# Weights and state-space parameters handed over in the layout in which the kernel loads them

## The chip, the core and the metric

The kernel runs on one core of one Trainium2 chip. The core has a matrix engine (TensorE, PE in the profile, with PEld for its weight loads), a vector engine (VectorE, DVE), a scalar engine (ScalarE, ACT), a general engine (GpSimd, POOL) and a queue engine (SyncE, SP). Sixteen DMA engines move data between HBM and the on-chip memory for the queues that SP, ACT and POOL fill. The metric is the device time of one execution in microseconds (us), the median over the runs.

## The reference, cut to what matters

One layer of a hybrid encoder over 16 meta tokens and 1024 tokens of width 1024, all in float32.

```
xn    = rmsnorm(h)                      # h = [meta; x], 1040 x 1024
proj  = xn @ w_in                       # 1024 x 4104: q 512, k 512, v 512, f 8, u 512, gates 2048
y_a   = forgetting_attention(q, k, v, f + b_forget) @ w_attn_out
z     = gelu(s5(u, lambda, b, c, d, log_dt))   # 32 groups, 64 complex states, 16 channels each
zg    = z @ w_glu ;  y_s = zg[:, :1024] * sigmoid(zg[:, 1024:])
h     = h + (sigmoid(gates_a) * y_a + sigmoid(gates_s) * y_s) @ w_o
hid   = rmsnorm(h) @ w_ffn_up           # 1024 x 5632
conv  = ffn_conv_b + causal depthwise conv of width 3 over hid
h     = h + (silu(conv_gate) * conv_val) @ w_ffn_down
out   = rmsnorm(h)[16:]
```

In the state-space part (S5) `lambda`, `b` and `c` are complex and come as real and imaginary arrays.

## The kernel before, in words

Every float32 product is computed as three products of a reduced-precision pair: an operand is split into `hi` (a cast) and `lo` (the rest, by `split_lo`, L128), and `dense_steps` (L142 to L146) issues hi\*hi, hi\*lo and lo\*hi. A weight chunk of 128 columns is loaded by `wchunk` (L130): one DMA of 512 KB into a tile `[128, 8, 128]`, whose DRAM side is a slice of the weight as the caller gave it, so 1024 pieces of 512 bytes. From `w_in` these pieces lie one row of 4104 floats, 16,416 bytes, apart.

The stages in order, and what of them matters here:

1. **Start (L255 to L302).** SP issues `x` (eight tiles of 512 KB, 4 KB per row), and after the second of them the four loads `uraw` (L288), 512 KB each, which bring the u columns of `w_in` in pieces of 2 KB. POOL loads lambda (`lraw`, four small DMAs, L1251) and `log_dt`. TensorE turns lambda to states-on-partitions (L1258), VectorE copies it out (L1259). ScalarE squares each token tile for its norm, VectorE scales it (L163), TensorE transposes it (L172), ScalarE and VectorE write `xhi` and `xlo` (L174, L128). `u_weights` (L269) splits the u weights on ScalarE and POOL.
2. **State-space stage (L304 to L342, function `ssm`).** A long chain of VectorE instructions builds tables from lambda, b and c; c is loaded in 256-byte pieces (L1267), transposed by eight TensorE instructions (L1452) and copied out by eight VectorE ones (L1455, L1457); b is loaded in 64-byte pieces (L1270, L1271). TensorE works on `u_proj` and on gate chunks (L372) meanwhile.
3. **z, q, k and the forget gate (L376 to L540).** The result of the state-space part goes to DRAM (`y_d`) and comes back (`zt`, L463). The 8 forget columns of `w_in` come as `fraw` (L383), 1024 pieces of 32 bytes, POOL splits them into `wf` (L386), and TensorE uses them at L438.
4. **Attention (L604 to L789).** Per pair of heads; between its products TensorE runs the next pair's q and k projection and gate chunks, whose weights come by `wchunk`. The attention output tile `ob` has one buffer; it is written by VectorE (L703) and stored by SP (L769).
5. Merge, output projection, feed-forward (L796 to L1221). `up_raw` (L926) loads 512 KB chunks of `w_ffn_up`. The convolution's parameters come in three loads, two TensorE transposes and a copy (L900 to L909).

A planner orders the instructions of each engine (`schedule_with_timeline_sim=True` in L1612) by planned times; engines then run their own lists in order, and so do the DMA queues. So a change of loads can also change the order.

Of the kernel before, what the change touches and what calls it, by code (L numbers as in the profile page):

```python
# [9 lines left out]
F = mybir.dt.float32  # L10
# [37 lines left out]
def block_kernel(ctx, tc, x, meta, g1, w_in, b_f, w_ao, l_re, l_im, b_re, b_im, c_re, c_im,  # L48
                 d_sk, l_dt, w_glu, w_o, g2, w_up, cw, cb, w_dn, gf, out, dbg=None, upto=99):
    nc = tc.nc  # L50
    dbg = dbg or {}
    x, g1, w_in, b_f, w_ao = x[0], g1[0], w_in[0], b_f[0], w_ao[0]
    l_re, l_im, b_re, b_im, c_re, c_im = l_re[0], l_im[0], b_re[0], b_im[0], c_re[0], c_im[0]
    d_sk, l_dt, w_glu, w_o, g2 = d_sk[0], l_dt[0], w_glu[0], w_o[0], g2[0]
    w_up, cw, cb, w_dn, out = w_up[0], cw[0], cb[0], w_dn[0], out[0]
# [225 lines left out]
    ssm_log, ssm_loads, ssm_steps = ssm(tc, after, sp, st_ps, ident, u_d, y_d, l_re, l_im, b_re, b_im, c_re, c_im, d_sk, l_dt)  # L281
# [207 lines left out]
    def glu(i):  # L489
# [64 lines left out]
    def value_weights(q):  # L554
# [6 lines left out]
        SY.dma_start(raw, w_in[2 * P * q:2 * P * q + 2 * P, 2 * AW:3 * AW].rearrange("(k p) m -> p k m", p=P))  # L561
# [338 lines left out]
    cwr = fc.tile([P, 2, P], F, name="cwr")  # L900
    cw2 = cw.rearrange("j (m p) -> (j m) p", p=P)
    SY.dma_start(cwr[:, 0], cw2[:P])
    SY.dma_start(cwr[:4, 1], cw2[P:])
    SY.dma_start(cwr[4:48, 1], cb.rearrange("(m p) -> m p", p=P))
    cwt = fc.tile([P, 176], F, name="cwt")
# [318 lines left out]
def ssm(tc, after, sp, s_ps, ident, u_d, y_d, l_re, l_im, b_re, b_im, c_re, c_im, d_sk, l_dt):  # L1224
# [6 lines left out]
    def TS(*a):  # L1231
        log.append(V.tensor_scalar(*a))
# [31 lines left out]
    def loads():  # L1264
        for w, (p0, p1) in enumerate(((c_re, c_im), (c_im, c_re))):
            for i, src in enumerate((p0, p1)):
                SY.dma_start(craw[:, :, w, i, :],  # L1267
                             src.rearrange("g c s -> (g c) s").rearrange("(m p) s -> p m s", p=P))
        for k_, (p0, p1) in enumerate(((b_re, b_im), (b_im, b_re))):
            SY.dma_start(bw[:64, k_], p0.rearrange("g s c -> s g c"))  # L1270
            SY.dma_start(bw[64:, k_], p1.rearrange("g s c -> s g c"))  # L1271
        SY.dma_start(dT, d_sk.rearrange("(g c) -> c g", c=GC))

    def rest():
# [173 lines left out]
        cA, cB = sm([P, G, GC]), sm([P, G, GC])  # L1448
        for mch in range(4):
            for w, dst in enumerate((cA, cB)):  # L1450
                tp = s_ps()
                PE.transpose(tp[:, :P], craw[:, mch, w].rearrange("p i s -> p (i s)"), ident)  # L1452
                dv = dst[:, 8 * mch:8 * mch + 8].rearrange("p g c -> p (g c)")
                if w == 0:
                    TS(dv, tp[:, :P], sg, None, ALU.mult)  # L1455
                else:
                    TS(dv, tp[:, :P], -1.0, None, ALU.mult)  # L1457
# [22 lines left out]
        def tables(qt):  # L1480
# [12 lines left out]
            TT(Gm, Gm, tm, ALU.add)  # L1493
# [122 lines left out]
```

## Time and profile before

| what | us |
|---|---|
| median of 3 runs | 1540.2 (1536.94 to 1541.24) |
| profiled execution, its own time | 1544.01 |
| its span from first to last instruction | 1542.1 |
| TensorE busy in the span | 1464.8 (95%) |
| mean granted TensorE clock | 0.984 of full speed |

The profile is of one execution, 3.8 us above the median of the timed runs. Busy times are read against the span; sums of changes are made against the execution's own time.

### The profile page before, as it was taken

To read this page: it belongs to the slowest core of one execution; us is meant where nothing else is said; L and a number is where in the kernel's file an instruction comes from. 1 tells how busy PE (TensorE), PEld (TensorE's weight loads), DVE (VectorE), ACT (ScalarE), POOL (GpSimd) and SP (SyncE) were. 2 spreads that over 40 slices of the span, in tenths; PEclk is the share of its full clock that TensorE was granted. 3 is DMA by queue.
4 is the path that set the end of the run, shared out by engine and by line. 5 is a ranking of instruction groups with operands and counts; after the bars stand their busy time and mean duration, and the time that the engine had idled before them with its cause. 6 is when DMAs were issued, how large, how long until landed. Compare 5 with 4: busy or idle time off the path is not lost.

```text
span 1542.1 us, 26276 instructions
## 1 busy us (share of the span) xinstructions
PE 1464.8 (95%) x9649; PEld 1373.3 (89%) x9649; DVE 1087.7 (71%) x2226; ACT 666.8 (43%) x1295; POOL 752.2 (49%) x810
## 2 busy tenths in 40 slices
PE   5998998999999989999999989999999999989997
PEld 4998897998899979999778989999999999878886
DVE  5999747882466656656425798888887774788695
ACT  5143456541455646542213444344444443454343
POOL 5332234853445445635201564555544336599766
PEclk9999998999999989999999999999999999999998
DMA  8466472553232233127542045667743224774412
GB/s 208 84 91 102 96 123 48 166 165 68 46 61 53 61 38 74 53 95 245 203 113 92 28 119 150 158 178 181 174 130 103 83 70 164 264 234 140 141 48 109
DMA packets 164450, 183.53 MB, mean 119 GB/s; under 512 B 25257, under 2 KB 120233, under 8 KB 163971
## 3 DMA queue, kind: packets, MB, share of 16 engines
q1 hardware_dynamic: 150883, 155.49, 35.4%
q0 software_dynamic: 7648, 15.78, 7.2%
q10 hardware_dynamic: 5792, 10.60, 1.9%
q8 instruction: 76, 1.25, 0.3%
q14 instruction: 51, 0.42, 0.1%
HBM read 142.76 MB, written 60.96 MB: 132 GB/s over the span
## 4 chain that ended last, share of the span: by engine, by line
PE 61%; DVE 19%; DMA 7%; issue 4%; POOL 4%; ACT 3%; SPq 1%; POOLq 0%; ACTq 0%; DVEq 0%
PE mm L146 4%; PE mm L144 4%; PE mm L145 4%; PE sp L200 3%; PE sp L201 3%; PE sp L202 3%; DVE sw L128 3%; PE tp L677 2%; PE tp L200 2%; PE tp L201 2%; PE tp L202 2%; DVE ov L1028 2%; PE mm L202 2%; PE mm L201 2%; PE mm L200 2%
## 5 line engine op out<-in xcount | busy, mean ns | idle before, releaser
L144 PE MATMUL mm<-xhi,whi 128*128 128x342 f32 (+2 forms) x584 | 192.6, 330 | 1.7 <-DVE q L128 1.0
L146 PE MATMUL mm<-xhi,wlo 128*128 128x342 f32 (+2 forms) x584 | 190.7, 327 | 0.0
L145 PE MATMUL mm<-xlo,whi 128*128 128x342 f32 (+2 forms) x584 | 190.3, 326 | 0.0
L144 PEld LDWEIGHTS mm<-xhi,whi 128*128 128x128 f32 x584 | 111.5, 191 | 3.5 <-ACT xhi L174 1.1
L128 DVE TENSOR_TENSOR sw<-sf,sw 128x512 fp32r<-128x512 f32 x76 | 75.1, 988 | 55.9 <-ACT sw L937 55.9
L968 POOL TENSOR_TENSOR ov<-ov,og 128x1024 f32<-128x1024 f32 x21 | 51.2, 2439 | 124.7 <-ACT og L967 121.9
L145 PEld LDWEIGHTS mm<-xlo,whi 128*128 128x128 f32 x584 | 111.4, 191 | 0.6 <-DVE xlo L128 0.2
L146 PEld LDWEIGHTS mm<-xhi,wlo 128*128 128x128 f32 x584 | 111.2, 191 | 0.6 <-issue 0.2
L128 POOL TENSOR_TENSOR wlo<-raw,whi 128x1024 fp32r<-128x1024 f32 x24 | 62.7, 2615 | 78.5 <-ACT whi L136 78.2
L937 ACT CAST sw<-sf 128x512 fp32r<-128x512 f32 x76 | 47.4, 624 | 117.7 <-POOL sf L945 92.2
L684 ACT CAST th<-tp 128x256 fp32r<-128x256 f32 (+3 forms) x120 | 56.1, 472 | 72.6 <-PE tp L677 29.5
L200 PE MATMUL mm<-xhi,sw 128*128 128x256 f32 (+1 forms) x304 | 85.5, 281 | 0.5 <-DVE ov L992 0.5
L202 PE MATMUL mm<-xhi,sw 128*128 128x256 f32 (+1 forms) x304 | 85.5, 281 | 0.0
L201 PE MATMUL mm<-xlo,sw 128*128 128x256 f32 (+1 forms) x304 | 85.2, 280 | 0.0
L128 DVE TENSOR_TENSOR tl<-tp,th 128x256 fp32r<-128x256 f32 (+3 forms) x120 | 65.2, 547 | 25.5 <-ACT th L684 23.7
L1028 DVE SCALAR_TENSOR_TENSOR ov<-hv,cwt,ov 128x1024 f32<-128x1024 f32 x38 | 77.7, 2043 | 1.9 <-ACT ov L1026 1.8
L945 POOL TENSOR_TENSOR sf<-raw 128x512 f32<-128x512 f32 x38 | 51.2, 1348 | 54.0 <-DVE hv L206 19.5
L945 POOL TENSOR_TENSOR sf<-raw,sf 128x512 f32<-128x512 f32 x38 | 67.1, 1766 | 21.3 <-DVE sw L128 21.3
L937 ACT CAST sw<-raw 128x512 fp32r<-128x512 f32 x69 | 42.4, 619 | 74.4 <-DMA raw<-in_w_ffn_up_dram 35.9
L649 POOL TENSOR_SCALAR pt<-pt,nm 128x144 f32<-128x144 f32 (+4 forms) x72 | 50.9, 709 | 43.6 <-DVE nm L648 42.4
L698 PE MATMUL po<-th,vt 128*128 128x256 f32 (+1 forms) x200 | 57.5, 302 | 7.9 <-DVE nm L645 7.8
L647 ACT ACTIVATE pt<-pt,nm 128x144 f32<-128x144 f32 (+4 forms) x72 | 52.9, 735 | 27.9 <-DVE nm L646 27.3
(603 smaller groups left out, 5467.8 us busy)
## 6 DMA issues: line engine op xcount, KB each, us to landing
raw<-in_w_ffn_up_dram SPq DMA_DIRECT2D x44, 512.0 KB, 4.0
t_d<-in_w_ffn_down_dram POOLq DMA_DIRECT2D x44, 256.0 KB, 6.9
ar<-a_d SPq DMA_DIRECT2D x44, 256.0 KB, 4.6
wr<-t_d SPq DMA_DIRECT2D x44, 256.0 KB, 2.9
a_d<-ov SPq DMA_DIRECT2D x21, 512.0 KB, 2.6
raw<-in_w_in_dram SPq DMA_DIRECT2D x20, 512.0 KB, 7.6
wr<-in_w_ffn_down_dram SPq DMA_DIRECT2D x33, 256.0 KB, 2.9
t_d<-in_w_ffn_down_dram SPq DMA_DIRECT2D x22, 256.0 KB, 4.7
```

What stands on the lines that cost most here:

```text
L128: return eng.tensor_tensor(out_, src, hi.bitcast(F), ALU.subtract)
L144: yield PE.matmul(ps, whi[:, i, :], ahi[:, i], start=(i == 0), stop=False)
L145: yield PE.matmul(ps, whi[:, i, :], alo[:, i], start=False, stop=False)
L146: yield PE.matmul(ps, wlo[:, i, :], ahi[:, i], start=False, stop=(i == k - 1))
L200: PE.matmul(ps, a[0][:, i], bh, start=(i == 0 and not joins), stop=False, skip_group_check=True)
L201: PE.matmul(ps, a[0][:, i], bl, start=False, stop=False, skip_group_check=True)
L202: PE.matmul(ps, a[1][:, i], bh, start=False, stop=(i == kh - 1), skip_group_check=True)
L684: S.copy(th[:kn, z:tw], tp[:kn, z:tw])
L698: PE.matmul(po[:, :w], vt[:kn, kk, h, :], th[:kn, gi * w:gi * w + w], start=(kk == 0), stop=False)
L937: S.copy(hi, src)
L945: sums.append(GP.tensor_tensor(f_, a, b, op))
L1028: V.scalar_tensor_tensor(out=o, in0=h_[:, j:SEQ + j], scalar=cwc(j, m), in1=o, op0=ALU.mult, op1=ALU.add)
```

## The change

The host now lays the inputs out before the kernel's DRAM tensors are made (`_laid_out`). The 128-column weights become blocks `[chunk, 128 partitions, k, 128]`, so a chunk is one run of 4 KB per partition (2 KB for `w_attn_out` and the halves of `w_glu`), 512 KB without gaps. The u and v columns become `[128, 8, 512]`, 16 KB per partition, of which each load takes 4 KB; the forget columns `[128, 8, 8]`. Lambda, b and c come with the states doubled over the 128 partitions, so that they are loaded as they are used, and the transposes of lambda, c and the convolution's parameters go. The sign of the second c array moves into `tables` (ADD becomes SUBTRACT). The lower half of the first u chunk's split moves from POOL to VectorE.

```diff
 def wchunk(src, k, eng=None, act=False):
-        (GP if act else SY).dma_start(raw, src.rearrange("(k p) m -> p k m", p=P))
+        (GP if act else SY).dma_start(raw, src)
...
-            split_lo(GP, lo[:, sl], src, hi[:, sl])
+            split_lo(V if m == 0 else GP, lo[:, sl], src, hi[:, sl])
...
-                SY.dma_start(raw, w_in[2 * P * j:2 * P * j + 2 * P, 3 * AW + H:3 * AW + H + SW]
-                             .rearrange("(k p) m -> p k m", p=P))
+                SY.dma_start(raw, w_u[:, 2 * j:2 * j + 2])
...
-        c0 = 3 * AW + H + SW + P * i
-        whi, wlo = wchunk(w_in[:, c0:c0 + P], KD, GP, act=not tanh)
+        whi, wlo = wchunk(w_g[i], KD, GP, act=not tanh)
...
-        SY.dma_start(fraw, w_in[:, 3 * AW:3 * AW + H].rearrange("(k p) m -> p k m", p=P))
+        SY.dma_start(fraw, w_f)
...
-            whi, wlo = wchunk(w_in[:, w * AW + P * pr:w * AW + P * pr + P], KD, GP)
+            whi, wlo = wchunk((w_q, w_k)[w][pr], KD, GP)
...
-            SY.dma_start(raw[:, 4 * q:4 * q + 4],
-                         w_glu[:, D * q + P * i:D * q + P * i + P].rearrange("(k p) m -> p k m", p=P))
+            SY.dma_start(raw[:, 4 * q:4 * q + 4], w_glu[KD * q + i])
...
-        SY.dma_start(raw, w_in[2 * P * q:2 * P * q + 2 * P, 2 * AW:3 * AW].rearrange("(k p) m -> p k m", p=P))
+        SY.dma_start(raw, w_v[:, 2 * q:2 * q + 2])
...
+            SY.dma_start(raw, w_o[4 * hf + m])
...
+        whi, wlo = wchunk(w_ao[i], 4)
...
-    tp = t_ps()
-    PE.transpose(tp[:, :P], cwr[:, 0], ident)
-    PE.transpose(tp[:, P:P + 48], cwr[:48, 1], ident[:48, :48])
-    V.tensor_copy(cwt, tp[:, :176])
+    cwt = fc.tile([P, 4, 2 * NFF], F, name="cwt")
+    SY.dma_start(cwt, cwt_d)
...
+        SY.dma_start(raw, w_up[m])
...
 def ssm(...):
-    lraw = big("dt8", [P, 2, 2, NS], "lraw")[:G]
-    for i, src in enumerate((l_re, l_im)):
-        for j in range(2):
-            GP.dma_start(lraw[:, i, j, :], src)
...
-    for i in range(2):
-        tp = s_ps()
-        PE.transpose(tp[:, :G], lraw[:, i].rearrange("g a s -> g (a s)"), ident[:G, :G])
-        V.tensor_copy(lam[:, i], tp[:, :G])
-    craw = big("tq", [P, 4, 2, 2, NS], "craw")
+    GP.dma_start(lam, lam_d)
+    cAB = sm([P, 2, G, GC])
...
+        SY.dma_start(cAB, cw_d)
+        SY.dma_start(bw, bw_d)
+        SY.dma_start(dT, d_sk)
...
-        for mch in range(4):
-            for w, dst in enumerate((cA, cB)):
-                tp = s_ps()
-                PE.transpose(tp[:, :P], craw[:, mch, w].rearrange("p i s -> p (i s)"), ident)
...
+        cA, cB = cAB[:, 0], cAB[:, 1]
+        TS(cA, cA, sg, None, ALU.mult)
...
-            TT(Gm, Gm, tm, ALU.add)
+            TT(Gm, Gm, tm, ALU.subtract)
...
+    def by_rows(w):
+        return w.reshape(-1, P, w.shape[1]).transpose(1, 0, 2)
+    def blocks(w):
+        return w.reshape(w.shape[0] // P, P, -1, P).transpose(2, 1, 0, 3)
+    def twice(re, im):
+        return _np.stack([_np.concatenate([re, im]), _np.concatenate([im, re])], axis=1)
```

## Rows read from the trace of the kernel before

**Rows 1.** The page's engines: busy us, share of the span, instructions.

```profile
PE 1464.8 (95%) x9649; PEld 1373.3 (89%) x9649; DVE 1087.7 (71%) x2226; ACT 666.8 (43%) x1295; POOL 752.2 (49%) x810
```

**Rows 2.** Waits of TensorE: for whom, us in total, times, longest us.

```profile
PE sp L1258 <- DMA lraw<-in_ssm_lambda_re_dram: 8.5, 1, 8.5
PE po L698 <- DVE nm L645: 7.8, 2, 6.9
...
PE tp L172 <- DVE sm L1259: 5.6, 1, 5.6
...
PE mm L438 <- DVE q L128: 4.4, 1, 4.4
```

**Rows 3.** Stretches of the start: busy us, instructions, clock, DMA share, GB/s.

```profile
8.00:17.00 9.00, 4.35 (x22) 3.70 (x22) 4.79 (x9) 4.47 (x11) 7.42 (x7) 1.00 0.96 185
17.00:27.00 10.00, 5.04 (x20) 4.42 (x21) 5.12 (x20) 5.78 (x12) 2.78 (x5) 1.00 1.05 367
```

**Rows 4.** The chain that ended last, its first long piece: start, us, what.

```profile
3.76 15.43 DMA uraw<-in_w_in_dram
```

**Rows 5.** Timeline of the start: start us, us, engine, line, what, idle before.

```profile
19.21 0.71 ACT L274 CAST whi<-uraw 128x256 fp32r<-128x256 f32 x2 [2.37 <-DMA uraw<-in_w_in_dram]
...
21.05 0.18 DVE L1259 COPY sm<-tp 128x32 f32<-128x32 f32 x1
...
21.28 1.12 PE L172 MATMUL tp<-ident,xt 128*128 128x128 f32 x4 [5.59 <-DVE sm L1259]
...
23.07 0.82 PE L144 MATMUL mm<-xhi,whi 128*128 128x272 f32 x2 [0.68 <-ACT xhi L174]
```

**Rows 6.** DMA issues from 543 to 558 us: KB each, us to landing.

```profile
raw<-in_w_in_dram SPq DMA_DIRECT2D x1, 512.0 KB, 13.0
o_d<-ob SPq DMA_DIRECT2D x1, 128.0 KB, 10.7
```

**Rows 7.** Timeline of the same stretch: SP's store, VectorE, TensorE.

```profile
547.09 12.99 SPq L769 DMA_DIRECT2D o_d<-ob  x2
...
557.84 0.17 DVE L703 TENSOR_TENSOR ob<-po,ot 64x16 f32<-64x16 f32 x1 [7.20 <-DMA o_d<-ob]
...
558.06 0.38 PE L698 MATMUL po<-th,vt 16*128 16x16 f32 x1 [6.86 <-DVE nm L645]
```

**Rows 8.** Stretches right after two stalls, columns as in rows 3.

```profile
558.00:564.00 6.00, 5.94 (x23) 5.92 (x24) 3.29 (x21) 2.63 (x8) 2.24 (x7) 0.52 0.02 3
...
248.40:256.60 8.20, 7.49 (x28) 6.08 (x29) 7.28 (x13) 7.71 (x19) 4.03 (x5) 0.50 0.07 20
```

**Rows 9.** Timeline around the forget gate: POOL, ACT, PE.

```profile
239.28 4.20 POOL L386 TENSOR_SCALAR wf<-fraw 128x64 fp32r<-128x64 f32 x1 [7.61 <-DMA fraw<-in_w_in_dram]
...
244.78 0.62 ACT L485 CAST z3h<-zf 128x520 fp32r<-128x520 f32 x1 [6.02 <-POOL zf L479]
...
248.41 0.46 PE L438 MATMUL mm<-xhi,wf 128*64 128x272 f32 x1 [4.44 <-DVE q L128]
```

**Rows 10.** The page's DMA issues: count, KB each, median us to landing.

```profile
raw<-in_w_ffn_up_dram SPq DMA_DIRECT2D x44, 512.0 KB, 4.0
...
raw<-in_w_in_dram SPq DMA_DIRECT2D x20, 512.0 KB, 7.6
```

**Rows 11.** Groups of instructions from 40 to 53 us: count, busy us, mean ns, idle.

```profile
L1232 DVE TENSOR_SCALAR sm<-sp,sm 128x128 f32<-128x128 f32 x4 | 1.4, 347 | 0.2 <-PE sp L1452 0.2
...
L1232 DVE TENSOR_SCALAR sm<-tp 128x128 f32<-128x128 f32 x4 | 1.1, 287 | 0.1
...
L1452 PE MATMUL tp<-ident,craw 128*128 128x128 f32 x4 | 1.1, 272 | 0.0
```

**Rows 12.** Single tiles, bw and raw: ns min/median/max, first and last start.

```profile
L1235 DVE TENSOR_TENSOR sm<-bw,sm x2: 678/678/679, 71.5 to 72.2; 128x512 f32<-128x512 f32 x2
...
L128 DVE TENSOR_TENSOR ops<-raw,ops x16: 388/668/941, 246.2 to 328.6; 128x256 fp32r<-128x256 f32 x16
```

**Rows 13.** A stretch of the state-space stage, columns as in rows 3.

```profile
120.00:140.00 20.00, 16.80 (x109) 16.22 (x109) 19.62 (x43) 6.93 (x10) 2.99 (x4) 0.91 0.62 125
```

More of the change, by code (lines that the diff above doesn't have):

```diff
@@ L47, in block_kernel @@
 @with_exitstack
-def block_kernel(ctx, tc, x, meta, g1, w_in, b_f, w_ao, l_re, l_im, b_re, b_im, c_re, c_im,
-                 d_sk, l_dt, w_glu, w_o, g2, w_up, cw, cb, w_dn, gf, out, dbg=None, upto=99):
+def block_kernel(ctx, tc, x, meta, g1, w_q, w_k, w_v, w_f, w_u, w_g, b_f, w_ao, lam_d, bw_d, cw_d,
+                 d_sk, l_dt, w_glu, w_o, g2, w_up, cwt_d, w_dn, gf, out, dbg=None, upto=99):
     nc = tc.nc
     dbg = dbg or {}
[L52 to L55, printed above, removed]
+    out = out[0]
     V, S, GP, PE, SY = nc.vector, nc.scalar, nc.gpsimd, nc.tensor, nc.sync
@@ L280, in block_kernel @@
     S.dma_start(g1B, g1.partition_broadcast(P))
-    ssm_log, ssm_loads, ssm_steps = ssm(tc, after, sp, st_ps, ident, u_d, y_d, l_re, l_im, b_re, b_im, c_re, c_im, d_sk, l_dt)
+    ssm_log, ssm_loads, ssm_steps = ssm(tc, after, sp, st_ps, ident, u_d, y_d, lam_d, bw_d, cw_d, d_sk, l_dt)
     xts = [sp.tile([P, D], F, tag=tag, name="xt", bufs=n) for tag, n in (("sy", 3), ("Gm", 2), ("Wi", 2), ("U", 2))
@@ L804, in wo_half @@
             raw = rp.tile([P, KD, P], F, tag=rtag, name="raw", bufs=1 if rtag == "wraw" else 2)
-            c0 = 512 * hf + P * m
-            SY.dma_start(raw, w_o[:, c0:c0 + P].rearrange("(k p) m -> p k m", p=P))
+            SY.dma_start(raw, w_o[4 * hf + m])
             sl = slice(P * m, P * m + P)
@@ L836, in block_kernel @@
         ga = ga if i < KD - 1 else okeep["g"]
-        whi, wlo = wchunk(w_ao[:, P * i:P * i + P], 4)
+        whi, wlo = wchunk(w_ao[i], 4)
         for t, n in QBLK:
@@ L899, in block_kernel @@
     fc = pool(st_r, "ffnc", side="right")
[L900 to L905, printed above, removed]
-    tp = t_ps()
-    PE.transpose(tp[:, :P], cwr[:, 0], ident)
-    PE.transpose(tp[:, P:P + 48], cwr[:48, 1], ident[:48, :48])
-    V.tensor_copy(cwt, tp[:, :176])
+    cwt = fc.tile([P, 4, 2 * NFF], F, name="cwt")
+    SY.dma_start(cwt, cwt_d)
     def cwc(j, m):
-        return cwt[:, 44 * j + m:44 * j + m + 1]
+        return cwt[:, j, m:m + 1]
     NH = LQ // 2 + 1
@@ L927, in up_raw @@
         raw = rp.tile([P, KD, P], F, tag="raw", name="raw", bufs=3)
-        SY.dma_start(raw, w_up[:, P * m:P * m + P].rearrange("(k p) m -> p k m", p=P))
+        SY.dma_start(raw, w_up[m])
         return raw
@@ L1221, in block_kernel, with ssm @@
         room[0] += len(groups[g])
-def ssm(tc, after, sp, s_ps, ident, u_d, y_d, l_re, l_im, b_re, b_im, c_re, c_im, d_sk, l_dt):
+def ssm(tc, after, sp, s_ps, ident, u_d, y_d, lam_d, bw_d, cw_d, d_sk, l_dt):
     nc = tc.nc
@@ L1264, in loads @@
     def loads():
[L1265 to L1272, printed above, removed]
+        SY.dma_start(cAB, cw_d)
+        SY.dma_start(bw, bw_d)
+        SY.dma_start(dT, d_sk)
     def rest():
@@ L1445, in rest @@
         yield
-        cA, cB = sm([P, G, GC]), sm([P, G, GC])
-        for mch in range(4):
-            for w, dst in enumerate((cA, cB)):
-                tp = s_ps()
-                PE.transpose(tp[:, :P], craw[:, mch, w].rearrange("p i s -> p (i s)"), ident)
[L1453 to L1457, printed above, removed]
+        cA, cB = cAB[:, 0], cAB[:, 1]
+        TS(cA, cA, sg, None, ALU.mult)
         b1, b2 = bw[:, 0], bw[:, 1]
@@ L1587, in ssm, with _laid_out @@
     return log, loads, rest()
-_INS = ["x", "meta_tokens", "norm_mix_g", "w_in", "b_forget", "w_attn_out", "ssm_lambda_re", "ssm_lambda_im",
-        "ssm_b_re", "ssm_b_im", "ssm_c_re", "ssm_c_im", "ssm_d", "ssm_log_dt", "w_glu", "w_o", "norm_ffn_g",
-        "w_ffn_up", "ffn_conv_w", "ffn_conv_b", "w_ffn_down", "norm_final_g"]
 _OUTS = [((1, SEQ, D), "float32")]
+def _laid_out(x, meta_tokens, norm_mix_g, w_in, b_forget, w_attn_out, ssm_lambda_re, ssm_lambda_im, ssm_b_re, ssm_b_im,
+              ssm_c_re, ssm_c_im, ssm_d, ssm_log_dt, w_glu, w_o, norm_ffn_g, w_ffn_up, ffn_conv_w, ffn_conv_b,
+              w_ffn_down, norm_final_g):
+    import numpy as _np
+    def by_rows(w):
[4 more added lines that the diff above has]
+        return _np.stack([_np.concatenate([re, im]), _np.concatenate([im, re])], axis=1)
+    w = w_in[0]
+    q, k, v, f, u, g = _np.split(w, [AW, 2 * AW, 3 * AW, 3 * AW + H, 3 * AW + H + SW], axis=1)
+    lam = _np.stack([ssm_lambda_re[0].T, ssm_lambda_im[0].T], axis=1)
+    conv = _np.concatenate([ffn_conv_w[0], ffn_conv_b], axis=0)
+    return dict(x=x[0], meta=meta_tokens, g1=norm_mix_g[0], w_q=blocks(q), w_k=blocks(k), w_v=by_rows(v),
+                w_f=by_rows(f), w_u=by_rows(u), w_g=blocks(g), b_f=b_forget[0], w_ao=blocks(w_attn_out[0]),
+                lam=_np.concatenate([lam, lam]),
+                bw=twice(ssm_b_re[0].transpose(1, 0, 2), ssm_b_im[0].transpose(1, 0, 2)),
+                cw=twice(ssm_c_re[0].transpose(2, 0, 1), ssm_c_im[0].transpose(2, 0, 1)),
+                d_sk=ssm_d[0].reshape(G, GC).T, l_dt=ssm_log_dt[0], w_glu=blocks(w_glu[0]), w_o=blocks(w_o[0]),
+                g2=norm_ffn_g[0], w_up=blocks(w_ffn_up[0]), cwt=conv.reshape(4, -1, P).transpose(2, 0, 1),
+                w_dn=w_ffn_down[0], gf=norm_final_g)
 def kernel(**inputs):
@@ L1604 @@
     arrays, args = {}, []
-    for name in _INS:
-        a = _np.ascontiguousarray(inputs[name])
+    for name, a in _laid_out(**inputs).items():
+        a = _np.ascontiguousarray(a)
         arrays[f"in_{name}_dram"] = a
```

## The prediction, made before the changed kernel ran

> **What bounds the kernel now.** I read the page's engines first [rows 1]: TensorE is busy 1464.8 of 1542.1 us, so all its idle time is 77 us, and no change of loads can win more than that, plus what the clock loses. So the question is not how many bytes or packets are saved but which of TensorE's pauses end with a load. The list of its waits [rows 2] names only four of 4 us or more that I can tie to this diff: 8.5 us for lambda and 5.6 us for the copy L1259, both at the start, 6.9 us at L698 in attention (the longest of two waits there), 4.4 us at L438. The list says which engine released TensorE, not what that engine had waited for; for that I went to the timeline around each, and to the chain that ended last for the start.
>
> At the start the chain holds one long piece, 15.43 us until the last `uraw` load lands at 19.2 us [rows 4]. The DMA engines are full all the while, but from 8 to 17 us, when u comes, they move 185 GB/s, and from 17 to 27 us, when mostly x follows, 367 [rows 3]. Bytes per time differ by two at the same busy share: it is how the u columns are read that is slow. ScalarE sits until that landing at 19.21 us and VectorE behind it, so the lambda copy runs only at 21.05 us and releases TensorE's transposes at 21.28; the first u product starts at 23.07 us [rows 5].
>
> In attention VectorE waits 7.20 us at L703 for the store of `ob`, which has one buffer, and TensorE 6.86 us behind it [rows 7]. That store, 128 KB, takes 10.7 us to land, and the load from `w_in` that was issued before it on SP takes 13.0 us for 512 KB [rows 6]. The store stands behind a slow load.
>
> At the forget gate POOL waits 7.61 us for `fraw`, spends 4.20 us on L386, and only then forms the sum for which ScalarE has waited 6.02 us; ScalarE's copies of q and VectorE's follow it, and TensorE stands 4.44 us at L438 [rows 9]. After either pause the granted clock is half for a while: 0.52 over 6 us and 0.50 over 8.2 us [rows 8].
>
> Loads from `w_in` are the slow ones: 7.6 us to land for 512 KB in 512-byte pieces, against 4.0 for `w_ffn_up` with the same pieces [rows 10].
>
> **The change part by part.**
>
> *Start.* Four u loads are 2.10 MB. At 185 GB/s that is 11.3 us, at the rate that x gets, 367 GB/s, 5.7 us: 5.6 us less. What is late next is the chain of norm and transposes of the second x tile; with lambda's transposes gone from TensorE and its two copies from VectorE nothing of [rows 5] but ScalarE's casts and `xlo` stands between that landing and the first product, so I let it move by the whole 5.6. The bound below is nothing: u is not contiguous after the change, its 4 KB pieces lie 16 KB apart. The 8.5 us of lambda [rows 2] I count at nothing more: it overlaps the wait for x and the u weights. The DMAs of b and c fall from eight to two and nothing in the list waits for them: zero.
>
> The split of the lower half of the first u chunk on VectorE is four instructions of 128x256. Such cost 0.39 to 0.67 us [rows 12], 1.6 to 2.7 us in all. VectorE is busy 4.79 of 9 us there [rows 3], so I take zero; if u lands in half the time and the cover is gone, 2.7 us at most.
>
> *Transposes.* Eight transposes of c at 0.272 us are at most 2.2 us of TensorE; eight copies on VectorE are 4 x 0.347 + 4 x 0.287 = 2.5 us [rows 11]. One multiply of 128x512 comes in. The trace has none from on-chip memory; bounds are 0.287 (the copy of 128 columns) and 0.678 (a two-operand instruction of that size [rows 12]); I take 0.5. VectorE is full in the stage that follows, 19.62 of 20 us while TensorE has 3.2 us idle [rows 13], so its time there is time of the end: 2.5 - 0.5 = 2.0 us; bounds 0 and 2.5. ADD against SUBTRACT, and the convolution's two transposes and copy far from any wait, are nothing.
>
> *Attention.* The chunk of q, k or gate weights becomes 512 KB without gaps. Even with the 4.0 us of `w_ffn_up`, still in 512-byte pieces in this trace [rows 10], the load issued at 543.5 us is done by 547.5, just after the store was issued at 547.09 us [rows 7], and the store no longer queues behind it. Won: 6.86 us, and of the six us at 0.52 of the clock 6 x 0.48 = 2.9 us [rows 8]; 9.7 together. I take 9.5; bound below 0, if another transfer stands there.
>
> *Forget gate.* `fraw` becomes 128 pieces of 256 bytes. It took 7.4 us from its issue to POOL's start. With 4 us [rows 10] POOL is 3.4 us earlier, and ScalarE and VectorE behind it. That leaves 1 us of the 4.44, and VectorE has work of its own in between. The clock's loss is 8.2 x 0.50 = 4.1 us [rows 8]. Bounds 0 and 8.5; I take 6, most of both.
>
> *Moved or shortened at no price.* The gate chunks' loads on POOL, the halves of `w_glu`, `w_o`, `w_attn_out` and `w_ffn_up` end earlier, but TensorE waits for none of them [rows 2]: zero, and no cover is needed as nothing is added to a queue. No instruction gains a wait that it did not have: each new DMA writes the tile that the old ones wrote.
>
> **Sum.** 5.6 + 2.0 + 9.5 + 6 = 23.1 us from 1544.01 us, the profiled execution's own time: 1520.9. That execution is 3.8 us above the median of 1540.2, inside what pauses of this kind can vary; I give **1520 us**, 1.3% less.
>
> **A rule that speaks against it.** The trace has 512-byte pieces at two speeds, 4.0 and 7.6 us for 512 KB [rows 10]. The Trainium skill, page "DMA: Bandwidth & Descriptors", section "Specifications", says that transfers reach line rate from 512 bytes up. By that rule longer rows win nothing, and only the transposes' 2.0 us stay: 1542 us. `w_ffn_up` agrees with the rule, `w_in` does not, so I hold that it is where the rows lie that slows `w_in`, and the sum does not go by it.
>
> **The rivals.**
>
> *u stays slow.* `w_in`'s rows are 16,416 bytes apart, and after the change u's pieces are 16,384 apart; if the distance is what is slow, the 5.6 us are not won: 1520 + 5.6 = 1525.6 us. For it: pieces of 2 KB are slow already. Against: nothing in the rows. The chunks of q, k and gates are free of it. The Trainium skill, page "DMA: Bandwidth & Descriptors", section "Latency and other measured facts", warns of row pitches at large powers of two; its figures begin at 512 KiB, so it says nothing for 16 KB, and no row here shows it.
>
> *Slower.* The exact 16 KB distance brings u to the worst rate seen, 512 KB in 13.0 us [rows 6], 40 GB/s. Then the four loads take 52 us and not 11.3, and the start is 41 us later: 1544 - 17.5 + 41 = 1567 us. It decides as soon as u's loss exceeds 17.5 + 4.6 us, that is beyond 33 us for 2.10 MB or below 63 GB/s. Against it: with rows of 16,416 bytes u had 185.
>
> *A new pause.* The planner orders all engines anew with other load times. One more pause like that of attention costs 6.86 + 2.9 = 9.7 us: 1530 us; two, 1539.5. For it: `ob` still has one buffer, and the clock falls after each pause. Against: the shorter the loads, the less a store can stand behind.
>
> *The layout does nothing.* If `w_in`'s loads were slow because of other traffic at those moments, all but the transposes stays: 1542 us. Against: at the start and in attention the traffic is different and both are slow.
>
> **How the numbers follow.** Likeliest, 0.55: 1520. u stays slow 0.12, one new pause 0.10, two 0.07, the layout does nothing 0.07, u at the worst rate 0.05, three or more pauses 0.04. This kernel's runs tell 0.3%, 4.6 us, from no change. Faster: 0.55 + 0.12 + 0.10 = 0.77. Same: 0.07 + 0.07 = 0.14. Slower: 0.05 + 0.04 = 0.09. The likeliest case's own range takes the bounds of its terms: with 5.6, 2.5, 9.7 and 8.5 won, and 3.8 for the median against the profile, 1514; with the forget gate's term at 0 and VectorE's split uncovered, 1529. The range of 8 in 10 reaches up to the two pauses, and down a little for loads that I counted at nothing: 1511 to 1538.
>
> **What would show it.** Start: the last `uraw` lands near 13.6 us and the first u product starts near 17.5. Attention: no VectorE wait at L703 above 2 us, no w_in load above 5 us, full clock around 550 us. Forget gate: POOL's wait for `fraw` under 4 us. State-space stage: no L1452, and one multiply near 0.5 us. Wrong if u still moves at 185 GB/s, or if TensorE's idle time, 77 us now, does not fall below 62.

## The result, and the profile after

| | us |
|---|---|
| after, median of 4 runs | 1514.86 (1513.86 to 1517.21) |
| before, median of 4 runs beside it | 1540.43 (1536.94 to 1541.24) |
| ratio | 0.984, 95% interval 0.9822 to 0.9859 |
| profiled execution after, its own time | 1513.86, span 1511.9, clock 0.991 |

The change makes the kernel faster by 1.6%, 25.6 us by the medians and 24.6 by the ratio (0.016 x 1540.4); 23.1 us were forecast. The two profiled executions lie 30.2 us apart, because the one of before was 3.8 us above its median and the one of after 1.0 below.

The page's engines and its line on DMA packets, answering to [rows 1]; last, the line on packets of before:

```profile
PE 1453.6 (96%) x9637; PEld 1366.8 (90%) x9637; DVE 1081.8 (72%) x2220; ACT 666.0 (44%) x1295; POOL 749.6 (50%) x803
...
DMA packets 81651, 183.53 MB, mean 121 GB/s; under 512 B 13466, under 2 KB 26410, under 8 KB 81172
```

```profile
DMA packets 164450, 183.53 MB, mean 119 GB/s; under 512 B 25257, under 2 KB 120233, under 8 KB 163971
```

TensorE's idle time is 1511.9 - 1453.6 = 58.3 us, from 77.3 (under 62 was forecast), and its busy time is 11.2 us less: twelve instructions at some 0.27 us [rows 11] are 3 of that, and the mean clock rose from 0.984 to 0.991. The packets fell from 164,450 to 81,651 for the same bytes. The experiments will show that this fall, the most visible number of the page, is not where most of the time came from.

The waits of TensorE, answering to [rows 2]; columns as there:

```profile
PE sp L169 <- DVE xm L160: 13.8, 1, 13.8
PE mm L972 <- DVE og L978: 7.3, 2, 4.5
PE sp L1488 <- DVE Vm L1221: 3.7, 2, 2.2
PE sp L1134 <- DVE u L1141: 3.6, 1, 3.6
PE tp L1467 <- DVE Gm L1221: 2.1, 1, 2.1
```

The 6.9 us in attention and the 4.4 us at the forget gate are gone. At the start 8.5 for lambda and 5.6 for its copy became one wait of 13.8 us for the first normed tile: nearly the same sum. What it stood behind is in the timeline of the start, answering to [rows 5]:

```profile
9.57 0.61 DVE L1218 TENSOR_SCALAR sm<-sm 128x32 f32<-128x32 f32 x3 [8.18 <-DMA sm<-in_l_dt_dram]
...
13.83 0.60 PE L169 MATMUL sp<-ident,xm 16*128 16x16 f32 x4 [13.83 <-DVE xm L160]
...
17.69 1.11 PE L169 MATMUL tp<-ident,xt 128*128 128x128 f32 x4 [0.61 <-DVE xt L160]
...
19.48 0.82 PE L141 MATMUL mm<-xhi,whi 128*128 128x272 f32 x2
```

The planner put the instructions on `log_dt` ahead of the norms in VectorE's list, and VectorE waited 8.18 us for that small load before it could scale the first tile. The first u product came at 19.48 us, not at the 17.5 forecast (23.07 before). The stretches that answer to [rows 3], and one around the place where attention paused before:

```profile
8.00:17.00 9.00, 2.92 (x16) 2.49 (x16) 7.15 (x27) 3.63 (x10) 3.50 (x5) 1.00 1.00 409
17.00:27.00 10.00, 7.98 (x34) 7.37 (x34) 9.92 (x36) 8.37 (x17) 4.68 (x6) 1.00 0.69 275
540.00:560.00 20.00, 20.00 (x141) 19.95 (x141) 15.22 (x62) 12.73 (x30) 10.67 (x21) 1.00 0.11 34
```

While u comes the DMA engines move 409 GB/s, from 185 before, and in attention TensorE is busy 20.00 of 20 us at full clock. The loads and the store from there, answering to [rows 6, 10]; count, KB each, median us to landing. Below them stand shortest, median and longest of all stores of `ob`, of after and then of before:

```profile
raw<-in_w_up_dram SPq DMA_DIRECT2D x44, 512.0 KB, 3.5
...
raw<-in_w_g_dram SPq DMA_DIRECT2D x8, 512.0 KB, 3.7
uraw<-in_w_u_dram SPq DMA_DIRECT2D x4, 512.0 KB, 10.5
raw<-in_w_q_dram SPq DMA_DIRECT2D x4, 512.0 KB, 4.4
...
o_d<-ob SPq DMA_DIRECT2D x12, 128.0 KB, 1.7
```

```profile
DMA to landing us min/median/max: 1.7/1.7/3.7
```

```profile
DMA to landing us min/median/max: 1.7/1.7/10.7
```

The chunks that took 7.6 us by the median land in 3.7 to 4.4. The median store of `ob` took 1.7 us before, too; what is gone is the late one of 10.7 us, and none takes longer than 3.7. At the forget gate, answering to [rows 9]:

```profile
230.00 0.69 POOL L381 TENSOR_SCALAR wf<-fraw 128x64 fp32r<-128x64 f32 x1
...
238.51 0.29 PE L433 MATMUL mm<-xhi,wf 128*64 128x272 f32 x1
```

POOL no longer waits for `fraw`, and its step takes 0.69 us and not 4.20. Last, four groups of products as marks of the stages: ns of one, then first and last start in the span.

```profile
L1545 PE MATMUL sp<-St,Gm x32: 272/275/350, 110.5 to 190.2; 128*128 128x130 f32 x32
...
L197 PE MATMUL sp<-z2h,ops x32: 277/282/285, 247.5 to 324.5; 128*128 128x260 f32 x32
...
L628 PE MATMUL sp<-k,q x120: 171/323/457, 330.6 to 646.2; 128*128 128x264 f32 x16, 128*128 128x328 f32 x16, 128*128 128x392 f32 x16, 128*128 128x456 f32 x16
...
L972 PE MATMUL mm<-xhi,sw x104: 313/320/623, 821.5 to 1280.9; 128*128 128x344 f32 x72, 128*128 128x342 f32 x32
```

The same groups in the trace of before give this table of where the 30.2 us came from:

| mark | before | after | ahead by |
|---|---|---|---|
| first state-space product with `St` | 123.1 | 110.5 | 12.6 |
| forget gate's first product | 248.4 | 238.5 | 9.9 |
| first product with `z2h` | 261.6 | 247.5 | 14.1 |
| last attention score `k,q` | 671.3 | 646.2 | 25.1 |
| first plain product of the feed-forward | 847.4 | 821.5 | 25.9 |
| last one | 1309.2 | 1280.9 | 28.3 |
| end of the span | 1542.1 | 1511.9 | 30.2 |

Of the 30.2 us, 4.6 are how far the two executions lie from their medians, and the marks don't tell in which stage. Three things are to be explained: 14 us up to z, 11 us in attention, and 2 to 4 us in the feed-forward stage, for which nothing was forecast. The lead of 12.6 us in the state-space stage is also striking: 2.7 of it are lost again by the forget gate.

### The profile page after: what moved, and what is told of

It is laid out like the page before. It is cut to its first block, busy times and chain, and to the rows that moved or that the text cites. A ratio compares the mean times of both kernels' runs of the same rounds, so it can differ in the third digit from the quotient of the medians.

```text
span 1511.9 us, 26231 instructions
## 1 busy us (share of the span) xinstructions
PE 1453.6 (96%) x9637; PEld 1366.8 (90%) x9637; DVE 1081.8 (72%) x2220; ACT 666.0 (44%) x1295; POOL 749.6 (50%) x803
## 2 busy tenths in 40 slices
DMA packets 81651, 183.53 MB, mean 121 GB/s; under 512 B 13466, under 2 KB 26410, under 8 KB 81172
## 4 chain that ended last, share of the span: by engine, by line
PE 75%; DVE 15%; issue 3%; POOL 3%; DMA 2%; ACT 2%; SPq 0%; POOLq 0%; DVEq 0%; ACTq 0%
PE mm L143 5%; PE mm L142 5%; PE mm L141 5%; PE sp L198 4%; PE sp L197 4%; PE sp L199 4%; PE tp L197 3%; PE tp L198 3%; PE tp L199 3%; PE tp L671 2%; PE mm L199 2%; PE mm L198 2%; PE mm L197 2%; PE po L693 2%; PE po L692 2%
## 5 line engine op out<-in xcount | busy, mean ns | idle before, releaser
L125 DVE TENSOR_TENSOR sw<-sf,sw 128x512 fp32r<-128x512 f32 x76 | 71.7, 944 | 53.4 <-ACT sw L923 53.2
L125 POOL TENSOR_TENSOR wlo<-raw,whi 128x1024 fp32r<-128x1024 f32 x24 | 69.2, 2886 | 56.4 <-ACT whi L133 40.2
L197 PE MATMUL mm<-xhi,sw 128*128 128x256 f32 (+1 forms) x304 | 85.4, 281 | 1.0 <-DVE ov L978 1.0
L125 DVE TENSOR_TENSOR tl<-tp,th 128x256 fp32r<-128x256 f32 (+3 forms) x120 | 65.2, 547 | 25.9 <-ACT th L678 24.6
L159 POOL TENSOR_TENSOR rs<-vr,nhalf 128x1 f32<-128x1 f32 (+2 forms) x18 | 10.2, 570 | 110.1 <-PE mm L875 52.4
```

The lines of the kernel that those rows point to most:

```text
L125: return eng.tensor_tensor(out_, src, hi.bitcast(F), ALU.subtract)
L197: PE.matmul(ps, a[0][:, i], bh, start=(i == 0 and not joins), stop=False, skip_group_check=True)
```

## The experiments

Ratios are against the kernel before on the same chip, whose median was 1538.47 to 1542.67 there. "From before" and "from after" say which kernel was edited.

### 1. The distance of the rows, the pieces as they were

The prediction held that `w_in` is slow for where its rows lie, 16,416 bytes apart. Three kernels change that distance; each load has the same number and length of pieces as before, and in all three traces every engine runs the same instructions in the same order as before (9649 on TensorE, 2226 on VectorE), and SP and ACT issue the same DMAs in the same order. So a new order by the planner is no rival here.

From before, the forget columns in an array of their own, so that rows are 16,384 bytes apart:

```diff
+    inputs["w_in"] = _np.concatenate([w_[:, :, :c_], w_[:, :, c_ + H:]], axis=2)
+    inputs["w_f"] = w_[:, :, c_:c_ + H]
```

> The kernel before, with the eight forget columns taken out of w_in into an array of their own, so that w_in's rows lie exactly 16,384 bytes apart and start on multiples of 64 bytes; the pieces of every load stay as long as before (512 bytes, 2 KB). Three theories of why w_in's loads are slow. Distance (rows about 16 KB apart): still slow, 1540 us, the chunk load near 543 us takes over 10 us, u moves near 185 GB/s. Start (rows of 16,416 bytes begin at odd multiples of 32 bytes): fast, u near 367 GB/s, no pause at L703, about 1520 us, since the order of work is that of before and only the start, the forget gate and attention gain. Length (the pieces are short): still slow, 1540 us.

From before, `w_in` padded with zero columns that nothing reads, to 17,440 bytes; like 16,416 an odd multiple of 32 bytes, so the rows start no better than before:

```diff
+    inputs["w_in"] = _np.concatenate([w_, _np.zeros((1, D, 4360 - w_.shape[2]), w_.dtype)], axis=2)
```

> The kernel before, with w_in padded by zero columns to 4360, so that its rows lie 17,440 bytes apart, away from 16 KB, but every second row still begins at an odd multiple of 32 bytes; all pieces as before. Distance: fast, about 1520 us. Start of the rows: still slow, 1540 us. Length: still slow, 1540 us.

The same with 4112 columns, 16,448 bytes, 32 more than before (one run):

```diff
+    inputs["w_in"] = _np.concatenate([w_, _np.zeros((1, D, 4112 - w_.shape[2]), w_.dtype)], axis=2)
```

> The kernel before, with w_in padded to 4112 columns: rows 16,448 bytes apart, 32 bytes more than before, each starting on a multiple of 64 bytes. If a distance a little over 16 KB is slow whatever the start of a row: about 1540 us, chunk loads from w_in above 7 us. If it takes both, near 16 KB and rows that start at odd multiples of 32 bytes: about 1519 us, chunk loads near 4.2 us.

Measured: 16,384 gives 1520.53 us, ratio 0.9886 (0.986 to 0.9913); 17,440 gives 1519.14, 0.9874 (0.9851 to 0.9896); 16,448 gives 1525.69 beside 1542.67 of before. The stretch of the start in which u comes, for 16,384, then 17,440, then 16,448:

```profile
8.00:17.00 9.00, 4.12 (x22) 3.49 (x22) 6.23 (x12) 5.68 (x15) 6.34 (x7) 1.00 1.04 364
```

```profile
8.00:17.00 9.00, 4.30 (x23) 3.67 (x23) 6.33 (x12) 5.65 (x15) 6.45 (x7) 1.00 1.03 368
```

```profile
8.00:17.00 9.00, 4.80 (x25) 4.12 (x26) 6.39 (x12) 5.24 (x15) 6.94 (x8) 1.00 1.03 370
```

All three move u at twice the 185 GB/s of [rows 3]. The 512 KB chunks in 512-byte pieces, of 17,440, then of 16,448:

```profile
raw<-in_w_in_dram SPq DMA_DIRECT2D x20, 512.0 KB, 4.2
```

```profile
raw<-in_w_in_dram SPq DMA_DIRECT2D x20, 512.0 KB, 4.6
```

They land in 4.2 and 4.6 us, from 7.6 [rows 10]. So the length of the pieces is not what made `w_in` slow. Nor is it alone that rows start at odd multiples of 32 bytes, for at 17,440 they do and are fast; nor is it alone that they lie close to 16 KB apart, for 32 bytes less or more than 16,416 are enough. Whether it takes both together, as the expectation of the third run had it, these distances don't separate: 16,416 is the only one of them that has both. The waits and the clock follow: with 17,440 the list of TensorE's waits has no pause at L698 and no 4.4 us at L438, and TensorE is busy all through the stretch where attention paused before:

```profile
540.00:560.00 20.00, 20.00 (x141) 19.95 (x140) 15.29 (x63) 12.56 (x30) 11.16 (x25) 1.00 0.12 34
```

And `fraw`, still in 1024 pieces of 32 bytes, was issued at 222.00 us and let POOL go at 224.74, in 2.7 us (7.4 before), in the timeline of that kernel:

```profile
224.74 4.22 POOL L386 TENSOR_SCALAR wf<-fraw 128x64 fp32r<-128x64 f32 x1 [2.00 <-DMA fraw<-in_w_in_dram]
...
237.50 0.29 PE L438 MATMUL mm<-xhi,wf 128*64 128x272 f32 x1
```

POOL's step takes 4.22 us here as in [rows 9], and the forget gate is as early as in the changed kernel. The products on `wf`, of before and then of this kernel, ns of one, first and last start:

```profile
L438 PE MATMUL mm<-xhi,wf x16: 332/386/460, 248.4 to 259.8; 128*64 128x272 f32 x8, 128*64 128x384 f32 x8
```

```profile
L438 PE MATMUL mm<-xhi,wf x16: 283/310/340, 237.5 to 246.3; 128*64 128x272 f32 x8, 128*64 128x384 f32 x8
```

From the first to the last it is 8.8 us and not 11.4, with the same work between. One line on the host that pads an array gives 1 - 0.9874, 1.26% or 19.4 us, of the change's 24.6 by its ratio.

The Trainium skill, page "DMA: Bandwidth & Descriptors", section "Specifications", gives 512 bytes as enough for line rate; at 17,440 bytes the runs agree (4.2 us in 512-byte pieces, 3.7 to 4.4 in 4 KB ones), at 16,416 they don't (7.6). The same page, section "Latency and other measured facts", tells of slow rows at large powers of two from 512 KiB up, and that a pad of 192 bytes did not help there; here the exact power of two, 16,384, is fast, and from 16,416 a pad of 32 bytes cures.

### 2. Does the distance slow another weight?

If it is the distance and not `w_in`, `w_ffn_up` must become slow by it. From after, `w_ffn_up` as two halves with rows of 2816 columns padded to 4104, so 16,416 bytes, in 512-byte pieces; and beside it the same pieces from the weight as the caller gave it, rows 22,528 bytes apart:

```diff
-        SY.dma_start(raw, w_up[m])
+        SY.dma_start(raw, w_up[m // NFF, :, P * (m % NFF):P * (m % NFF) + P].rearrange("(k p) m -> p k m", p=P))
```

> The changed kernel, with w_ffn_up as two halves of 2816 columns, each padded by zeros to 4104, so that its rows lie 16,416 bytes apart and its 44 loads come in 512-byte pieces, as w_in's did. If the distance is the cause, whichever tensor has it: these loads land in 7 us or more and not in 3.5 to 4.0, and the feed-forward stage, which hides most of it, loses 5 to 20 us, 1520 to 1535 us. If it was something of w_in itself (where it lies, what runs beside it): landing 4 us, within 3 us of the run with w_ffn_up's rows as before.

```diff
-        SY.dma_start(raw, w_up[m])
+        SY.dma_start(raw, w_up[:, P * m:P * m + P].rearrange("(k p) m -> p k m", p=P))
```

> The changed kernel, with w_ffn_up read in 512-byte pieces from rows 22,528 bytes apart, as before. If its long rows gave the 2 to 5 us that the changed kernel has over row distance alone: 1518 us. If not: 1515 us, since no wait of TensorE ended with these loads.

Measured: at 16,416 bytes 1584.57 us, ratio 1.0294 (1.0278 to 1.031); at 22,528 bytes 1520.11, 0.987 (0.9855 to 0.9886). The load of the first kernel, one of its waits, and a stretch of its feed-forward stage; each is followed by that of the second:

```profile
raw<-in_w_up_dram SPq DMA_DIRECT2D x44, 512.0 KB, 9.9
```

```profile
raw<-in_w_up_dram SPq DMA_DIRECT2D x44, 512.0 KB, 4.3
```

```profile
PE sp L197 <- DVE u L203: 36.5, 13, 7.8
```

```profile
900.00:1200.00 300.00, 268.27 (x2115) 265.91 (x2115) 196.55 (x267) 108.42 (x175) 132.66 (x103) 0.93 0.70 136
```

```profile
900.00:1200.00 300.00, 297.76 (x2484) 295.92 (x2484) 243.40 (x312) 127.48 (x207) 148.87 (x115) 1.00 0.57 147
```

The distance carries the slowness with it: 9.9 us and not 4.3. It costs 64.5 us, far more than the 5 to 20 expected, and the order of work is not the reason: both kernels run the same instructions in the same order as the changed one. 44 loads are slow, TensorE waits 36.5 us for VectorE at L197 (products whose operand `sw` is made from these weights), is busy 268 of 300 us and not 298, and its clock falls to 0.93. The stage has one such load per 10 us of TensorE's work, and one takes 9.9 us: that leaves no slack to hide in.

### 3. The parts of the change, undone or alone

The q, k and gate chunks back to `w_in`, from after:

```diff
-            whi, wlo = wchunk((w_q, w_k)[w][pr], KD, GP)
+            whi, wlo = wchunk(w_in[:, c0:c0 + P].rearrange("(k p) m -> p k m", p=P), KD, GP)
```

> The changed kernel, with the chunks of q, k and the gates read from w_in as before, in 512-byte pieces 16,416 bytes apart. If these loads made the pause in attention and the late z stage: 9.5 to 16 us slower than the changed kernel, 1524 to 1531 us, with a long wait for the store of ob again. Rival, that the new order of the planner removed the pauses: 1512 to 1518 us.

Measured: 1533.19 us, ratio 0.9958 (0.9944 to 0.9971), 18 us of the gain lost, a little more than the 16 expected at most. Its loads, VectorE's line in the timeline of attention, and the products on `wf`:

```profile
raw<-in_w_in_dram SPq DMA_DIRECT2D x16, 512.0 KB, 7.7
```

```profile
548.16 0.17 DVE L699 TENSOR_TENSOR ob<-po,ot 64x16 f32<-64x16 f32 x1 [6.01 <-DMA o_d<-ob]
```

```profile
L435 PE MATMUL mm<-xhi,wf x16: 283/310/340, 243.9 to 251.0; 128*64 128x272 f32 x8, 128*64 128x384 f32 x8
```

The loads are at 7.7 us again, and VectorE stands 6.01 us for the store of `ob` at the same instruction as in [rows 7]. The order of work is that of the changed kernel but for six places on TensorE and eight on POOL, which leaves the rival little room. And not all of the loss is in attention: the forget gate's first product comes at 243.9 us and not 238.5, although `fraw` comes as in the changed kernel; 5.4 us are lost there by the chunks alone, and by the last attention score it is 15.6 (661.8 against 646.2).

The u columns back to `w_in`, from after; and, the other way round, u alone laid out, from before:

```diff
-                SY.dma_start(raw, w_u[:, 2 * j:2 * j + 2])
+                SY.dma_start(raw, w_in[2 * P * j:2 * P * j + 2 * P, 3 * AW + H:3 * AW + H + SW]
+                             .rearrange("(k p) m -> p k m", p=P))
```

> The changed kernel, with u read from w_in as before. If the start moves by what u's load takes longer: 5.6 us slower, 1520.5 us. If VectorE's idle time before 40 us is what counts, because VectorE sets the end of the state-space stage: 5 to 9 us slower. Rival, that the wait for log_dt which now stands ahead of the norms hides u: 1513 to 1517 us.

```diff
-                SY.dma_start(raw, w_in[2 * P * j:2 * P * j + 2 * P, 3 * AW + H:3 * AW + H + SW]
-                             .rearrange("(k p) m -> p k m", p=P))
+                SY.dma_start(raw, w_u[:, 2 * j:2 * j + 2])
```

> The kernel before, with u alone in the changed layout. The prediction's term for the start: 5.6 us faster than before. If the state-space stage swallows an earlier start, as putting u back into the changed kernel cost nothing: first u product 4 to 5 us earlier, but within 2 us of before at the end.

Measured: u back costs nothing clear of the intervals, 1514.42 us, 0.9838 (0.9817 to 0.9859). Alone it gives 1536.91, 0.9981 (0.997 to 0.9992), 2.9 us, between the two expectations. The first u product of either, first start after "x584":

```profile
L141 PE MATMUL mm<-xhi,whi x584: 283/321/592, 21.4 to 667.0; 128*128 128x342 f32 x109, 128*128 128x384 f32 x63, 128*128 128x272 f32 x23
```

```profile
L144 PE MATMUL mm<-xhi,whi x584: 282/321/689, 19.2 to 684.3; 128*128 128x342 f32 x109, 128*128 128x384 f32 x63, 128*128 128x272 f32 x23
```

With u slow again the first product comes at 21.4 us and not 19.5, but the forget gate's first product at 238.2 and not 238.5, in the same order of work: no time of the end hangs on these 2 us.

The weights alone, from before, with parameters and transposes as they were; and from after all weights as the caller gave them, but `w_in` with rows of 17,440 bytes, so that of the change the parameters and transposes stay:

```diff
-        (GP if act else SY).dma_start(raw, src.rearrange("(k p) m -> p k m", p=P))
+        (GP if act else SY).dma_start(raw, src)
...
+    inputs.update(w_q=blocks(q), w_k=blocks(k), w_v=by_rows(v), w_f=by_rows(f), w_u=by_rows(u), w_g=blocks(g))
+    for n_ in ("w_attn_out", "w_glu", "w_o", "w_ffn_up"):
+        inputs[n_] = blocks(inputs[n_][0])
```

> The kernel before with all weights in the changed kernel's layout, and lambda, b, c and the convolution's parameters loaded and transposed as before. If the rest comes from long rows: 1515 us. If it comes from the parameters and the transposes: 1519 us, the same as row distance alone. The prediction's term for the transposes, 2.0 us, would put it at 1517.

```diff
-        SY.dma_start(raw, w_up[m])
+        SY.dma_start(raw, w_up[:, P * m:P * m + P].rearrange("(k p) m -> p k m", p=P))
...
-                w_q=blocks(q), w_k=blocks(k), w_v=by_rows(v),
-                w_f=by_rows(f), w_u=by_rows(u), w_g=blocks(g), b_f=b_forget[0], w_ao=blocks(w_attn_out[0])
+                w_in=_np.concatenate([w, _np.zeros((D, 4360 - w.shape[1]), w.dtype)], axis=1),
+                b_f=b_forget[0], w_ao=w_attn_out[0]
```

> The changed kernel with its state-space and convolution parameters, but with all weights read as before in pieces of 512 bytes to 2 KB, and w_in's rows 17,440 bytes apart. If what is left between row distance alone (1519.1 us) and the whole change (1514.9) comes from the parameters and the transposes: 1515 us. If it comes from long rows, above all of w_ffn_up: 1519 us.

Measured: the weights alone 1518.34 us, 0.9844 (0.9831 to 0.9858), as good as the whole change (0.984). With the parameters and no long rows 1520.14, 0.9862 (0.9844 to 0.9879), and without the parameters, in experiment 1, 0.9874. On either ground what the parameters and transposes give, 0.6 and 1.8 us by the ratios, is within the intervals, which are too wide to rule out 2 us. The first product with `St` comes at 110.5 us with them and at 117.9 without. Why so little of that is left, two stretches show; first of the weights alone, then of the changed kernel, both up to the forget gate's first product, which comes at 238.5 us in either:

```profile
19.00:110.00 91.00, 85.87 (x552) 81.58 (x552) 89.07 (x300) 37.23 (x77) 31.09 (x39) 0.96 0.45 102
110.00:238.50 128.50, 119.86 (x803) 117.20 (x802) 101.45 (x148) 59.33 (x94) 40.72 (x24) 0.99 0.36 103
```

```profile
19.00:110.00 91.00, 83.76 (x525) 80.36 (x523) 90.02 (x288) 38.15 (x78) 31.27 (x42) 0.98 0.35 93
110.00:238.50 128.50, 122.76 (x823) 120.47 (x824) 98.92 (x149) 62.96 (x104) 45.06 (x25) 0.99 0.37 109
```

TensorE's idle time in the two stretches is 5.1 + 8.6 = 13.8 us with the weights alone and 7.2 + 5.7 = 13.0 after. The earlier state-space work only changes places with gate chunks; the sum of TensorE's work up to the forget gate is nearly the same.

The wait for `log_dt` at the start, from after, with it and lambda loaded by SP ahead of x:

```diff
-    GP.dma_start(ldt, l_dt.partition_broadcast(P))
+    SY.dma_start(ldt, l_dt.partition_broadcast(P))
...
-    GP.dma_start(lam, lam_d)
+    SY.dma_start(lam, lam_d)
```

> The changed kernel, with log_dt and lambda loaded by SP ahead of x and not by POOL. VectorE waits 8.2 us for log_dt at the start of the changed kernel, and the norms stand behind it in its order. If this wait moves the start: first u product 3 us earlier, near 16.5 us, and 3 us less, 1512 us. Rival, that the first u product waits for x, g1 and u whatever VectorE does: within 1 us of the changed kernel.

Measured: 1519.93 us, 0.9851 (0.9837 to 0.9865); a miss, nothing won. TensorE's wait at L169 fell from 13.8 to 9.8 us, but the first u product came at 19.3 us, 0.2 earlier, and the forget gate at 245.1 us, 6.6 later. Here the planner did reorder all engines, so this run tests the wait and a new order at once; it does not show that the wait for `log_dt` held the first u product.

### 4. The feed-forward weights, and two edits in place of the change

Experiment 2 left a remainder: at 22,528 bytes, a distance at which loads are fast, 512-byte pieces give 0.987 against 0.984, though the intervals overlap. So the last kernel takes before with two edits only, `w_in` padded to 17,440 bytes and `w_ffn_up` in blocks:

```diff
+    inputs["w_in"] = _np.concatenate([w_, _np.zeros((1, D, 4360 - w_.shape[2]), w_.dtype)], axis=2)
+    inputs["w_ffn_up"] = _np.asarray(inputs["w_ffn_up"])[0].reshape(KD, P, -1, P).transpose(2, 1, 0, 3)
```

> The kernel before with two edits of layout alone: w_in padded so that its rows lie 17,440 bytes apart, and w_ffn_up in blocks, 4 KB per partition. If row distance and the long rows of w_ffn_up are all that the change wins: a ratio to before of 0.984, about 1515 us, as the whole change. If long rows in one tensor win nothing by themselves and the rest was the new order: 0.9874, about 1519 us, as row distance alone.

Measured: 1516.53 us (1513.62 to 1518.71), 0.9849 (0.9829 to 0.9869): within the intervals as good as the whole change, with the instructions of before in the order of before. The plain products of the feed-forward, first and last start, of this kernel and then of the one with short pieces at 22,528:

```profile
L986 PE MATMUL mm<-xhi,sw x104: 313/320/492, 824.6 to 1284.0; 128*128 128x344 f32 x72, 128*128 128x342 f32 x32
```

```profile
L972 PE MATMUL mm<-xhi,sw x104: 313/320/626, 822.8 to 1286.0; 128*128 128x344 f32 x72, 128*128 128x342 f32 x32
```

459.4 us from first to last against 463.2. The same row of all kernels, the one at 16,416 bytes left out: with `w_ffn_up` in blocks (after and five experiments) 457.5 to 461.4 us, mean 459.4; in short pieces (before and six) 461.8 to 465.7, mean 463.4. The two groups don't overlap in 13 traces, though only 0.4 us lies between them. By these traces the long rows of `w_ffn_up` are worth about 4.0 us; the times of single kernels are too coarse to show it. About half of it stands in one wait of TensorE, the one that grew to 36.5 us in experiment 2; here of before, then of after:

```profile
PE sp L200 <- DVE u L206: 2.2, 4, 0.7
```

```profile
PE sp L197 <- DVE u L203: 0.4, 1, 0.4
```

In the seven kernels with short pieces it is 1.1 to 3.5 us, mean 2.1, in the six with blocks at most 0.6.

No kernel here is faster than the change beyond the intervals.

## Why the prediction came out, step by step

**Where the rows lie: right, and sharper than I had it.** The prediction set the two speeds of 512-byte pieces against each other and held that `w_in` is slow for where its rows lie. Experiments 1 and 2 show it: with the same work in the same order, changing the distance alone gives 19.4 us (95% interval 16.0 to 22.9), and another weight laid at that distance becomes slow. The rival that the layout does nothing is out, and so are those by which u at exactly 16 KB stays slow or falls to the worst rate: the changed kernel moved u at 409 GB/s, and the first kernel of experiment 1, at 16,384 bytes as well, at 364.

**Attention, 9.5 us: right.** From the first product with `z2h` to the last score the kernel is 25.1 - 14.1 = 11.0 us faster. With the order of before and 17,440 bytes it is (671.3 - 261.6) - (647.4 - 248.1) = 10.4. The store no longer waits behind a slow load, the full clock stays, and undoing the chunks brings the pause of 6.01 us back. No new pause came.

**Forget gate, 6 us: the size about right, the step wrong.** The step said that `fraw` comes sooner because it is 128 pieces and not 1024. With 1024 pieces at 17,440 bytes it came in 2.7 us, the 4.4 us at L438 went all the same, and the products on `wf` were through 11.4 - 8.8 = 2.6 us sooner: 7.0 us. The pieces were not the cause; the distance was, and not that of `fraw` alone: with `fraw` as in the changed kernel and only the chunks slow, 5.4 us were lost by this point.

**Start, 5.6 us: mis-sized.** The rate doubled as forecast (409 GB/s), but the last `uraw` lands at 3.4 + 11.5 = 14.9 us, its issue and the longest of the four times to landing: 4.3 us sooner than the 19.2 of before, where 13.6 was forecast. And the first product gained only 3.6 us. The step said that nothing but ScalarE's casts and `xlo` stands after that landing; in the timeline above the transposes of the second x tile stand there, at 17.69 us, behind VectorE's norm of it. That the order behind `log_dt` made this later is argued and not shown. Alone the u layout is worth 2.9 us (95% interval 1.2 to 4.6), and undone in the changed kernel nothing. The prediction named that chain as late next and then let the product "move by the whole 5.6" all the same; and by the experiment with u back, 2 us at the start are gone again by the forget gate.

**Transposes, 2.0 us: not seen.** L1452 is gone and the multiply took 478 ns, for 0.5 forecast. But the argument "VectorE is full there, so its time is time of the end" doesn't hold in the traces: TensorE had gate chunks to do in the meantime, and its idle time up to the forget gate is nearly the same with and without (13.0 and 13.8 us). The multiply, in the groups of VectorE from 30 to 60 us of the changed kernel:

```profile
L1218 DVE TENSOR_SCALAR sm<-sm,sm 128x512 f32<-128x512 f32 x1 | 0.5, 478 | 0.0
```

**`w_ffn_up`, counted at zero: about 4.0 us.** "TensorE waits for none of them" was read from the list of waits, which names engines and not loads: ScalarE and POOL prepare these chunks and wait for them, TensorE's waits on VectorE come after. Of the about 4 us some 2 stand in the list of waits of before, as 2.2 us at L200 for VectorE's `u`, below the 4 us at which the prediction's reading of that list stopped; where the rest is was not followed.

So the sum of 23.1 came close to the 25.6 measured (24.6 by the ratio) partly by luck, by errors that nearly cancel: 5 to 8 us too much at the start and for the transposes, 4 too little in the feed-forward stage, 1.5 in attention and 1 at the forget gate. What was not luck is the mechanism and the choice of where it pays. The parts are 19.4 us for the row distance, by the ratio, and about 4 for `w_ffn_up`, by the traces; together, in one kernel, 1.51% or 23.3 us.

**What stays open.** Why 16,416 bytes is slow, and whether other distances are, above all others close to 16 KB with rows that start at odd multiples of 32 bytes; none was tried. Why 16,448 gained 17.0 us and 17,440 more was seen in one run only and may be scatter.

## What to carry to other kernels

When one tensor's loads take twice as long as another's with pieces of the same length, change the distance of its rows first: a pad on the host is one line and here gave four fifths of a large rewrite. A slow load is to be looked for also where no engine waits for it: here one of 13.0 us stood ahead of a store that took 10.7 instead of 1.7, the buffer of that store held VectorE and TensorE for 7 us, and the clock fell to half afterwards. An earlier end of a side chain is worth something only if the busiest engine has nothing else to do at that point: compare its idle time up to the next point that both kernels must pass, not the chain's end.

## What the runs showed of the hardware

- At a row distance of 16,416 bytes loads ran at about half rate: u at 185 GB/s against 364, 370 and 368 at 16,384, 16,448 and 17,440 bytes; 512 KB in 512-byte pieces in 7.6 us against 4.2 to 4.6; the same of `w_ffn_up` in 9.9 us against 4.3 at 22,528.
- Away from that distance the length of the pieces did less: 512 KB of `w_ffn_up` landed in 3.5 to 3.7 us in 4 KB pieces (six kernels) and in 3.9 to 4.5 in 512-byte ones (seven).
- At the start, while SP's loads fill the DMA engines, VectorE waited 8.18 us for a load of `log_dt` on POOL's queue.
- POOL's step on `wf`, the same instruction on 128x64 elements, took 4.20 us in the kernel before, 4.22 at 17,440 bytes, 2.72 at 16,448, 3.81 with the two edits, and 0.69 in the changed one. No run told why.
